# Weight rows of the channel mixers read by TensorE as several regions in turn

## The chip, the cores and the metric

The kernel runs on one core of a Trainium2 chip. The metric is the device time of one execution in microseconds (us). Before the change the median of three runs is 2255.92 us (2255.71 to 2256.01).

## The reference

A decoder trunk of two layers over 256 tokens of 2048 features, in float32. Layer 0 mixes tokens by gated linear attention, layer 1 by forgetting attention; each also attends to 256 memory tokens, and each ends in a channel mixer, the part that this change is about:

```python
def conv_ffn(h, w_up, conv_w, conv_b, w_down):
    u = causal_dwconv(h @ w_up, conv_w, conv_b)
    a, val = split_cols(u, [FFN_HIDDEN, FFN_HIDDEN])
    return (jax.nn.silu(a) * val) @ w_down

def reference(...):
    ...
        h = rmsnorm(x, norm_ffn[i])
        x = x + conv_ffn(h, ffn_w_up[i], ffn_conv_w[i], ffn_conv_b[i], ffn_w_down[i])
```

FFN_HIDDEN is 5632, so h @ w_up is a product of 256 x 2048 by 2048 x 11264, and the second one of 256 x 5632 by 5632 x 2048.

## The kernel before

**A product from three.** TensorE multiplies in the type fp32r. To keep float32's precision, each operand is split into a high part, rounded to fp32r, and a low part, what is left. The activations lie split in SBUF: bufA and bufB, 16 tiles each of 128 features x (high, low) x 256 tokens. A weight tile comes in float32 (raw), ScalarE rounds it (whi, L206), and VectorE takes the difference (wlo, L215). products() (L219 to L231) then adds three matmuls per block of 128 tokens and 128 features into a PSUM bank: high activations by high weights (L227), low activations by high weights (L228), and, behind all of these, high activations by low weights (L231).

**What a matmul reads.** The activations (128 features x 128 tokens) are the stationary operand. The weights are the moving operand: the matmul reads a row of n columns, 512 in the channel mixers, from each of 128 partitions of whi or wlo, from the first column to the last, and writes a row of n columns of PSUM per token.

**Units and panels.** _panels() lists all weights as panels of up to 512 columns, and the host lays them out so that a unit of two blocks of 128 input features by n columns is one DMA of 512 KB (n = 512), 128 partitions x 1024 floats. split_unit() issues load, rounding and difference of a unit; the pools hold four raw tiles, three whi and three wlo. proj_tm() runs one panel through all its units; proj_two() runs two panels side by side. Each unit is used for two blocks of tokens, so a unit is 2 x 2 x 3 = 12 matmuls. The columns of a panel of the form "turned" or "four" are placed by the host in the order SPREAD, so that what comes out of PSUM can be turned on VectorE; that order is the same before and after.

**The channel mixer** (ffn, L864) works in three parts of the hidden features, PARTS = ((0, 16), (16, 32), (32, 44)) in blocks of 128. In each part come the "up" panels (a pair of blocks of both halves each: 8, 8 and 6 panels of 16 blocks of input features), with the convolution and the gate behind them on ScalarE and VectorE, and then four "down" panels (of 16, 16 and 12 blocks), whose results add_out() adds to x on VectorE. Per layer that is 768, 384, 768, 384, 576 and 288 matmuls, in this order. Layer 0's mixer reads bufB for "up" and bufA for "down", layer 1's the other way round. The "down" panels of the last part of layer 1 are the end of the program, before the final norm and the store.

**split()** (L371 to L382) writes a row of 256 tokens as high and low part. With dealt set, it reads its source straight on and writes every other token to the first and to the second half of the row in turn (128 floats apart); without, it writes straight on.

The order of instructions on each engine comes from the program's order and a scheduler with priorities; every weight DMA is on SyncE's queue.

Of the kernel before, what the change touches and what calls it, by code (L numbers as in the profile page):

```python
# [31 lines left out]
PARTS = ((0, 16), (16, 32), (32, 44))  # L32
# [23 lines left out]
def _panels():  # L56

    full = list(range(KC))  # L60
    out = []

    def tm(key, w, c0, n, kcs=full, more=()):
        out.append((key, w, kcs, [(c0, n), *more], 2))

    def turned(key, w, blocks, kcs=full):

        out.append((key, w, kcs, [(blocks, 512)], 2))

    def four(key, w, c0, kcs=full):  # L70
        turned(key, w, [c0 + k * P for k in range(4)], kcs)

    for l in range(2):
        four(("mk", l), ("mem_w_kv", l), 0)
        tm(("mv", l), ("mem_w_kv", l), 512, 512)
    for h in range(GLA_H):
        tm(("gv", h), ("gla_w_in", 0), G_V + h * DV, DV, more=[] if h else [(G_R, RANK)])
        turned(("qk", h), ("gla_w_in", 0), [g + h * DK + k * P for g in (G_Q, G_K) for k in range(2)])
    for j in range(3):
        four(("og", j), ("gla_w_in", 0), G_OG + j * 512)  # L80
    four(("mq", 0), ("gla_w_in", 0), G_MQ)
    late = list(range(12, 16)) + list(range(12))

    def ffn(l):
        for p, (lo, hi) in enumerate(PARTS):
            for j in range(lo, hi, 2):
                turned(("up", l, j), ("ffn_w_up", l), [c + k * P for c in (0, HID) for k in (j, j + 1)])
            for f in range(4):
                four(("down", l, p, f), ("ffn_w_down", l), f * 512, list(range(lo, hi)))

    for f in range(4):
        four(("wo", 0, f), ("gla_w_out", 0), f * 512)
    ffn(0)
    for j in range(3):
        four(("fk", j), ("fox_w_kv", None), F_K + j * 512)
    for j, (lo, hi) in enumerate(FV_PARTS):
        more = [] if j else [(F_L, FOX_H)]
        tm(("fv", j), ("fox_w_kv", None), F_V + lo, hi - lo, more=more)
    four(("mq", 1), ("fox_w_in", 0), FOX_H * HD)
    for j in range(3):  # L100
        four(("fq", j), ("fox_w_in", 0), j * 512)
    for f in range(4):
        four(("wo", 1, f), ("fox_w_out", 0), f * 512, late)
    ffn(1)
    return out


def _layout():

    where, off = {}, 0  # L110
    for key, _, kcs, cols, per in _panels():
        n = sum(c[1] for c in cols)
        units = []
        for u in range(0, len(kcs), per):
            units.append((off, kcs[u : u + per], n))
            off += P * per * n
        where[key] = units
    return where, off
# [17 lines left out]
def _trunk(ctx: ExitStack, tc: tile.TileContext, xt, xtok, memt, wp, wgu, gns, gfin, cnv, par, msk, out):  # L136
    nc = tc.nc
    where, _ = _layout()
    V, S, TE = nc.vector, nc.scalar, nc.tensor
# [69 lines left out]
    def split_unit(unit, pieces=1, before=None, pool=wpool):  # L209
        with tc.high_priority(offset=AHEAD):  # L210
            raw, hi, w = load_unit(unit, pieces, before, pool)
            lo = pool.tile([P, NUNIT], F32R, name="wlo", tag="wlo", bufs=3)
            for i in range(pieces):
                s = slice(i * w // pieces, (i + 1) * w // pieces)
                V.tensor_tensor(lo[:, s], raw[:, s], hi[:, s].bitcast(F32), ALU.subtract)  # L215
        passed()
        return hi, lo

    def products(accs, src, base, unit, hi, lo, first, last):  # L219

        kcs, n = unit[1], unit[2]
        low = []
        for b, acc in accs:
            for j, kc in enumerate(kcs):
                s = slice(j * n, (j + 1) * n)
                xh, xl = (src[kc - base][:, i, b * P : (b + 1) * P] for i in range(2))
                TE.matmul(acc[:, :n], xh, hi[:, s], start=first and j == 0, stop=False)  # L227
                TE.matmul(acc[:, :n], xl, hi[:, s], start=False, stop=False)  # L228
                low.append((acc[:, :n], xh, lo[:, s], last and j == len(kcs) - 1))
        for a, xh, ls, stop in low:  # L230
            TE.matmul(a, xh, ls, start=False, stop=stop)  # L231

    def proj_tm(key, src, evac, spare=None, before=None):

        units = where[key]
        n = units[0][2]
        base = min(min(u[1]) for u in units)
        acc = [pacc.tile([P, 512], F32, name="acc", tag="acc") for _ in range(2)]
        ahead = 0 if spare is None else 4
        ready = {}  # L240
        for i in range(len(units) + ahead):
            if i < len(units):
                pool = wpool if spare is None or i < 3 else spare
                ready[i] = split_unit(units[i], pool=pool) if before is None else before(i, units[i])
            for bs, u in [((0, 1), i)] if not ahead else [((0,), i), ((1,), i - ahead)]:
                if 0 <= u < len(units):
                    products([(b, acc[b]) for b in bs], src, base, units[u], *ready[u], u == 0, u == len(units) - 1)
                    if u == len(units) - 1:
                        for b in bs:
                            evac(b, acc[b][:, :n])  # L250

    def proj_two(keys, src, evacs, late):

        units = [where[k] for k in keys]
        base = min(min(u[1]) for u in units[0])
        acc = [[pacc.tile([P, 512], F32, name="acc", tag="acc") for _ in range(2)] for _ in keys]
        count = len(units[0])
        for part in (range(count - late), range(count - late, count)):
            for i in range(2):
                for u in part:  # L260
                    unit = units[i][u]
                    hi, lo = split_unit(unit)
                    products(list(enumerate(acc[i])), src, base, unit, hi, lo, u == 0, u == count - 1)
                if part[-1] == count - 1:
                    for b in range(2):
                        evacs[i](b, acc[i][b][:, : units[i][0][2]])
# [240 lines left out]
    with tc.tile_pool(name="load", bufs=1) as lp:  # L507
# [31 lines left out]
        def mv_out(l):  # L539
            return to_values(nrm, 512, lambda c: mv[l][:, c, :])  # L540

        proj_tm(("mk", 0), bufA, keys(0), before=first)
        nc.sync.dma_start(mask[:, :M_SCAN], msk[:, :M_SCAN])
        sq, acc = [x[f].rearrange("p b (c t) -> p (b c) t", t=T) for f in range(2)]
# [9 lines left out]
        with tc.issue_after(loads[-1].ins):  # L554
            for i in range(KC):
                nc.sync.dma_start(xf[i], xt[i])
            nc.sync.dma_start(part, par)
            nc.sync.dma_start(mask[:, M_SCAN:], msk[:, M_SCAN:M_FOX])
        proj_tm(("mv", 0), bufA, mv_out(0))
        for i in range(KC):  # L560
            split(bufB, i, xf[i], gain("mix0", i), False)
        proj_tm(("mk", 1), bufA, keys(1))
        with tc.issue_after(loads[-1].ins):
            for f in range(4):
# [186 lines left out]
    def fox(nx, kept, then):  # L751
        hk, hq, mix = bufB, bufA, bufB
        with tc.tile_pool(name="fox", bufs=1) as fp:
# [6 lines left out]
            def keys(j):  # L760
                return to_features([(0, 4, nx.col)], lambda: lambda k: kt[:, 4 * j + k, :])

            proj_two([("fk", j) for j in range(2)], hk, [keys(j) for j in range(2)], 2)

            def queries(f):
# [85 lines left out]
    def add_out(key, src, then=None, spare=None, late=1):  # L851
        def evac(f):
            def out(b, a):
                V.tensor_tensor(x[f][:, b, :], x[f][:, b, :], a, ALU.add)  # L854
                if then is not None:
                    then(f, b)

            return out

        proj_two([(*key, f) for f in range(2)], src, [evac(f) for f in range(2)], late)  # L860
        for f in range(2, 4):
            proj_tm((*key, f), src, evac(f), spare if f == 3 else None)
# [54 lines left out]
    def preparing(name, dst):  # L917
        n = StreamNorm()
        turns = {}

        def then(f, b):
            n.add(f, b)
            if not b:
                turns[f] = Turn("xturned", 4)
            turns[f].put(b, x[f][:, b, :])
            if not b:
                return

            def halves(c):
                def step(t):  # L930
                    for k in (c, c + 1):
                        split(dst, 4 * f + k, t[:, k, :], gain(name, 4 * f + k))

                return step

            transfers(turns[f], back, (9, halves(0)), (10, halves(2)))

        return n, then, turns

    n, then, _ = preparing("ffn0", bufB)  # L940
# [3 lines left out]
    n, then, _ = preparing("ffn1", bufA)  # L944
# [121 lines left out]
```

## Time and profile before

| | |
|---|---|
| runs: median (lowest to highest) | 2255.92 us (2255.71 to 2256.01) |
| the profiled execution's own time | 2254.47 us |
| its span, first to last instruction | 2252.7 us |
| TensorE busy | 2239.9 us, 99% |
| VectorE busy | 1525.7 us, 68% |
| ScalarE busy | 1276.5 us, 57% |
| DMA | 516.96 MB, mean 229 GB/s |
| mean granted TensorE clock | 0.999 |

The tables of the profile name an engine (PE is TensorE's matmuls, PEld its weight loads, DVE VectorE, ACT ScalarE, POOL GpSimd, SP SyncE), a line of the kernel, and out<-in with the program's names and shapes. "x768" is a count; "174.10 (x769)" is busy us and instructions; in a row of a group, the numbers behind the bar are busy us and mean ns of one, then the idle time before it and who ended it. Matmuls overlap in TensorE, so the mean ns of one is longer than the time from one start to the next. Times in stretches are us from the span's start. A row that is timed "A:B" is such a stretch.

### The profile page before, as it was taken

To read this page: it belongs to the slowest core of one execution; us is meant where nothing else is said; L and a number is where in the kernel's file an instruction comes from. 1 tells how busy PE (TensorE), PEld (TensorE's weight loads), DVE (VectorE), ACT (ScalarE), POOL (GpSimd) and SP (SyncE) were. 2 spreads that over 40 slices of the span, in tenths; PEclk is the share of its full clock that TensorE was granted. 3 is DMA by queue.
4 is the path that set the end of the run, shared out by engine and by line. 5 is a ranking of instruction groups with operands and counts; after the bars stand their busy time and mean duration, and the time that the engine had idled before them with its cause. 6 is when DMAs were issued, how large, how long until landed. Compare 5 with 4: busy or idle time off the path is not lost.

```text
span 2252.7 us, 29275 instructions
## 1 busy us (share of the span) xinstructions
PE 2239.9 (99%) x10336; PEld 1874.8 (83%) x10336; DVE 1525.7 (68%) x2317; ACT 1276.5 (57%) x1850; POOL 2.9 (0%) x15
## 2 busy tenths in 40 slices
PE   9999999999999999999999999999999999999998
PEld 7888888888888888888888998888888888888886
DVE  7568988667675576646776556766776467664766
ACT  7555666556553565535665655555655456544654
POOL 0000000000000000000000000000000000000000
PEclk9999999999999999999999999999999999999999
DMA  9875666677775777657777876677776677766774
GB/s 318 279 233 188 207 204 220 205 233 246 250 234 195 227 237 246 209 195 247 234 250 255 257 266 202 181 251 238 244 251 216 196 240 240 242 203 210 239 242 150
DMA packets 303771, 516.96 MB, mean 229 GB/s; under 512 B 178556, under 2 KB 187272, under 8 KB 303496
## 3 DMA queue, kind: packets, MB, share of 16 engines
q1 hardware_dynamic: 124296, 427.24, 57.1%
q10 hardware_dynamic: 179328, 87.85, 13.9%
q8 instruction: 81, 1.33, 0.2%
q14 instruction: 66, 0.54, 0.1%
HBM read 470.44 MB, written 44.58 MB: 229 GB/s over the span
## 4 chain that ended last, share of the span: by engine, by line
PE 98%; DMA 1%; DVE 1%; issue 0%; ACT 0%; SPq 0%; DVEq 0%; ACTq 0%
PE acc L227 32%; PE acc L228 32%; PE acc L231 31%; DMA raw<-wp 0%; PE ps_s L683 0%; PE ps_s L485 0%; PE ps_t L478 0%; PE ps_o L496 0%; DMA xf<-xt 0%; DVE wlo L215 0%; DMA back<-turned 0%; PE ps_s L825 0%; PE ps_o L841 0%; PE ps_o L703 0%; PE ps_s L603 0%
## 5 line engine op out<-in xcount | busy, mean ns | idle before, releaser
L215 DVE TENSOR_TENSOR wlo<-raw,whi 128x1024 fp32r<-128x1024 f32 (+4 forms) x809 | 969.7, 1201 | 636.6 <-ACT whi L206 615.4
L206 ACT ACTIVATE whi<-raw 128x1024 fp32r<-128x1024 f32 (+4 forms) x809 | 842.3, 1043 | 860.0 <-PE acc L228 703.3
L227 PE MATMUL acc<-whi,B 128*128 128x512 f32 (+3 forms) x1792 | 685.7, 384 | 0.0
L228 PE MATMUL acc<-whi,B 128*128 128x512 f32 (+3 forms) x1792 | 684.5, 383 | 0.0
L227 PE MATMUL acc<-whi,A 128*128 128x512 f32 x1440 | 562.3, 392 | 1.4 <-ACT A L378 1.0
L228 PE MATMUL acc<-whi,A 128*128 128x512 f32 x1440 | 559.8, 390 | 0.0
L231 PE MATMUL acc<-wlo,B 128*128 128x512 f32 (+3 forms) x1792 | 469.3, 382 | 0.0
L231 PE MATMUL acc<-wlo,A 128*128 128x512 f32 x1440 | 387.2, 390 | 0.3 <-DVE wlo L215 0.3
L227 PEld LDWEIGHTS acc<-whi,B 128*128 128x128 f32 x1792 | 336.3, 188 | 60.5
L228 PEld LDWEIGHTS acc<-whi,B 128*128 128x128 f32 x1792 | 336.0, 188 | 59.5
L231 PEld LDWEIGHTS acc<-wlo,B 128*128 128x128 f32 x1792 | 333.7, 188 | 59.7
L227 PEld LDWEIGHTS acc<-whi,A 128*128 128x128 f32 x1440 | 270.6, 188 | 60.0 <-ACT whi L206 1.8
L228 PEld LDWEIGHTS acc<-whi,A 128*128 128x128 f32 x1440 | 270.7, 188 | 55.9 <-DVE A L382 0.2
L231 PEld LDWEIGHTS acc<-wlo,A 128*128 128x128 f32 x1440 | 270.0, 188 | 56.6 <-DVE wlo L215 0.7
L881 ACT ACTIVATE cv<-u,cw 128x256 f32<-128x256 f32 x176 | 96.9, 589 | 22.9 <-DMA u<-turned 22.9
L882 DVE SCALAR_TENSOR_TENSOR cv<-u,cw,cv 128x256 f32<-128x256 f32 x176 | 78.2, 479 | 14.9 <-ACT cv L881 14.9
L298 DVE STREAM_TRANSPOSE square<-scaled 128x512 f32<-128x512 f32 x122 | 80.0, 691 | 0.0
L883 DVE SCALAR_TENSOR_TENSOR cv<-u,cw,cv 128x256 f32<-128x256 f32 x176 | 77.1, 479 | 0.0
L854 DVE TENSOR_TENSOR x<-x,acc 128x512 f32<-128x512 f32 x64 | 41.2, 681 | 22.7 <-PE acc L231 22.7
L896 ACT ACTIVATE scaled<-acc,ny 128x512 f32<-128x512 f32 x88 | 54.8, 674 | 0.0
L462 ACT ACTIVATE sq<-x 128x256 f32<-128x256 f32 x80 | 32.5, 408 | 15.4 <-DVE x L854 14.0
L886 DVE TENSOR_TENSOR cv<-cv,cv 128x256 f32<-128x256 f32 x88 | 37.3, 424 | 1.4 <-ACT cv L885 1.4
(179 smaller groups left out, 846.3 us busy)
## 6 DMA issues: line engine op xcount, KB each, us to landing
raw<-wp SPq DMA_DIRECT2D x743, 512.0 KB, 4.2
turned<-square ACTq DMA_DIRECT2D x61, 512.0 KB, 4.5
u<-turned ACTq DMA_DIRECT2D x176, 128.0 KB, 5.2
raw<-wp SPq DMA_DIRECT2D x32, 384.0 KB, 3.1
raw<-wp SPq DMA_DIRECT2D x24, 388.0 KB, 4.5
back<-xturned ACTq DMA_DIRECT2D x64, 128.0 KB, 5.1
xturned<-square ACTq DMA_DIRECT2D x12, 512.0 KB, 4.4
back<-turned ACTq DMA_DIRECT2D x32, 128.0 KB, 4.2
```

The source lines that it names most:

```text
L206: casts.append(S.activation(hi[:, s], raw[:, s], AF.Copy))
L215: V.tensor_tensor(lo[:, s], raw[:, s], hi[:, s].bitcast(F32), ALU.subtract)
L227: TE.matmul(acc[:, :n], xh, hi[:, s], start=first and j == 0, stop=False)
L228: TE.matmul(acc[:, :n], xl, hi[:, s], start=False, stop=False)
L231: TE.matmul(a, xh, ls, start=False, stop=stop)
L298: V.transpose(self.square[:, :, :, b], src.rearrange("p (c t) -> p c t", t=32))
L854: V.tensor_tensor(x[f][:, b, :], x[f][:, b, :], a, ALU.add)
L881: S.activation(r, v[:, 2:], AF.Identity, bias=w[3], scale=w[2])
L882: V.scalar_tensor_tensor(r, v[:, 1 : T + 1], w[1], r, ALU.mult, ALU.add)
L883: V.scalar_tensor_tensor(r, v[:, :T], w[0], r, ALU.mult, ALU.add)
L886: V.tensor_tensor(cv[1], cv[0], cv[1], ALU.mult)
L896: S.activation(e, a, AF.Copy, scale=nx.col()[:, b : b + 1])
```

## The change

A table gives a form (s, t) for each part of each layer's "up" and "down" panels. The row of 512 floats is taken as s regions of 512 / s floats. A matmul reads t floats from the first region, t from the second, and so on through all s, then the next t of the first. The host places the columns so that what is read in this order is what was read straight on before; so PSUM gets the same columns in the same order, and the results are as before. All three matmuls read so. ScalarE and VectorE still write whi and wlo straight on, the DMAs are the same in number, size and order, and on every engine the same instructions stand in the same order with the same waits. The other panels (attention, memory, their output projections) have no form and are read straight on.

| part | up, layer 0 | down, layer 0 | up, layer 1 | down, layer 1 |
|---|---|---|---|---|
| 0 | 2 regions, runs of 16 | 4, 16 | 2, 32 | 8, 4 |
| 1 | 2, 4 | 2, 8 | 2, 128 | 8, 16 |
| 2 | 2, 64 | 4, 4 | 4, 32 | 2, 2 |

```diff
+RUNS = {
+    ("up", 0, 0): (2, 16), ("up", 0, 1): (2, 4), ("up", 0, 2): (2, 64),
+    ("down", 0, 0): (4, 16), ("down", 0, 1): (2, 8), ("down", 0, 2): (4, 4),
+    ("up", 1, 0): (2, 32), ("up", 1, 1): (2, 128), ("up", 1, 2): (4, 32),
+    ("down", 1, 0): (8, 4), ("down", 1, 1): (8, 16), ("down", 1, 2): (2, 2),
+}
+
+
+def _runs(key):
+    if key[0] == "up":
+        key = (*key[:2], next(p for p, (lo, hi) in enumerate(PARTS) if lo <= key[2] < hi))
+    return RUNS.get(key[:3])
...
-    def products(accs, src, base, unit, hi, lo, first, last):
+    def products(accs, src, base, unit, hi, lo, first, last, runs=None):
 
         kcs, n = unit[1], unit[2]
+
+        def moving(t):
+            return t if runs is None else t.rearrange("p (s g t) -> p g s t", s=runs[0], t=runs[1])
+
         low = []
         for b, acc in accs:
             for j, kc in enumerate(kcs):
                 s = slice(j * n, (j + 1) * n)
                 xh, xl = (src[kc - base][:, i, b * P : (b + 1) * P] for i in range(2))
-                TE.matmul(acc[:, :n], xh, hi[:, s], start=first and j == 0, stop=False)
-                TE.matmul(acc[:, :n], xl, hi[:, s], start=False, stop=False)
-                low.append((acc[:, :n], xh, lo[:, s], last and j == len(kcs) - 1))
+                TE.matmul(acc[:, :n], xh, moving(hi[:, s]), start=first and j == 0, stop=False)
+                TE.matmul(acc[:, :n], xl, moving(hi[:, s]), start=False, stop=False)
+                low.append((acc[:, :n], xh, moving(lo[:, s]), last and j == len(kcs) - 1))
...
             at = np.empty(512, np.int64)
             at[SPREAD] = np.concatenate([np.arange(c, c + P) for c in cols[0][0]])
+            if _runs(key) is not None:
+                s, r = _runs(key)
+                at = at.reshape(-1, s, r).transpose(1, 0, 2).reshape(-1)
             blk = w3[kcs][:, :, at]
```

proj_tm() and proj_two() pass the form of their panel to products().

More of the change, by code (lines that the diff above doesn't have):

```diff
@@ L246, in proj_tm @@
                 if 0 <= u < len(units):
-                    products([(b, acc[b]) for b in bs], src, base, units[u], *ready[u], u == 0, u == len(units) - 1)
+                    products([(b, acc[b]) for b in bs], src, base, units[u], *ready[u], u == 0, u == len(units) - 1, _runs(key))
                     if u == len(units) - 1:
@@ L262, in proj_two @@
                     hi, lo = split_unit(unit)
-                    products(list(enumerate(acc[i])), src, base, unit, hi, lo, u == 0, u == count - 1)
+                    products(list(enumerate(acc[i])), src, base, unit, hi, lo, u == 0, u == count - 1, _runs(keys[i]))
                 if part[-1] == count - 1:
```

## The prediction

> **What bounds the kernel now.** First the page of the profile: the busy time of each engine, and the chain that ended last.
>
> ```profile
> PE 2239.9 (99%) x10336; PEld 1874.8 (83%) x10336; DVE 1525.7 (68%) x2317; ACT 1276.5 (57%) x1850; POOL 2.9 (0%) x15
> ...
> PE 98%; DMA 1%; DVE 1%; issue 0%; ACT 0%; SPq 0%; DVEq 0%; ACTq 0%
> PE acc L227 32%; PE acc L228 32%; PE acc L231 31%; DMA raw<-wp 0%; PE ps_s L683 0%; PE ps_s L485 0%; PE ps_t L478 0%; PE ps_o L496 0%; DMA xf<-xt 0%; DVE wlo L215 0%; DMA back<-turned 0%; PE ps_s L825 0%; PE ps_o L841 0%; PE ps_o L703 0%; PE ps_s L603 0%
> ```
>
> The chain is TensorE's own queue: 98% of it, and 95% are the three matmuls of products(), the lines that the diff edits. A busy TensorE says little by itself, so the next view is the table of stretches of time, cut where the timeline shows products() change from one buffer of activations to the other: the twelve parts of the channel mixers in their order (layer 0 up, down, up, down, up, down, then layer 1). Columns: stretch, its length, busy time and instructions of TensorE, of its weight load, of VectorE and of ScalarE, GpSimd, granted clock, DMA share, GB/s.
>
> ```profile
> 469.80:643.90 174.10, 174.10 (x769) 144.14 (x768) 124.61 (x186) 105.13 (x147) 0.00 (x0) 1.00 0.75 242
> 643.90:730.94 87.04, 87.04 (x385) 72.10 (x384) 49.34 (x55) 39.30 (x44) 0.00 (x0) 1.00 0.62 206
> 730.94:905.02 174.08, 174.08 (x769) 144.19 (x768) 118.90 (x163) 100.50 (x134) 0.00 (x0) 1.00 0.73 235
> ...
> 992.06:1122.62 130.56, 130.56 (x577) 108.14 (x576) 87.75 (x119) 74.12 (x98) 0.00 (x0) 1.00 0.73 233
> 1122.62:1187.90 65.28, 65.28 (x289) 54.07 (x288) 46.94 (x62) 39.57 (x68) 0.31 (x1) 1.00 0.80 255
> ...
> 1698.88:1785.92 87.04, 87.04 (x385) 72.10 (x384) 49.36 (x55) 39.29 (x44) 0.00 (x0) 1.00 0.64 206
> ...
> 2177.60:2243.10 65.50, 65.50 (x289) 53.90 (x287) 43.59 (x62) 35.80 (x65) 0.00 (x0) 1.00 0.52 169
> ```
>
> Busy time equals length in every row: TensorE has no hole, at a granted clock of 1.00. The pace is the same everywhere: 174.08 / 768 = 87.04 / 384 = 65.28 / 288 = 0.2267 us from one matmul's start to the next. So no weight tile is late, VectorE and ScalarE are done early (124.6 and 105.1 of 174.1 us at most), and any nanosecond that a matmul gains or loses here reaches the end in full. The view of waits agrees; TensorE's two largest in the whole span are
>
> ```profile
> PE ps_o L172 <- DVE B L169: 1.4, 1, 1.4
> PE acc L227 <- ACT A L378: 1.0, 2, 0.7
> ```
>
> of which the first is before any product. A stretch of the forgetting layer with 384 columns per matmul splits the pace into its parts (16.67 us for 96 matmuls):
>
> ```profile
> 1304.60:1321.27 16.67, 16.67 (x98) 16.67 (x97) 9.40 (x10) 8.51 (x11) 0.00 (x0) 1.00 0.90 303
> ```
>
> 16.67 / 96 = 173.6 ns for 384 columns against 226.7 for 512: (226.7 - 173.6) / 128 = 0.415 ns per column, and 226.7 - 512 x 0.415 = 14 ns that do not depend on the width. TensorE takes a float from each row of the weight tile every 0.415 ns.
>
> **The change part by part.** Every instruction stays in its place on its engine, with its waits; the weight DMAs (512 KB each), the split on ScalarE and VectorE and the writes to PSUM keep their shapes. Only the order in which a matmul reads its 512 weights differs: by the table of stretches, 768 + 384 + 768 + 384 + 576 + 288 = 3168 matmuls per layer, 6336 in all, 1436 us of the 2252.7. All else I cost at nothing: the host's new column order is no device time, and the loads and splits that hide behind TensorE now would hide better behind a slower one. If TensorE became faster, VectorE's 124.6 of 174.1 us leaves room for 28%.
>
> The price of a jump between regions is not in the trace for these matmuls. The one TensorE operation that reads two runs (L636, runs of 64 columns) stands beside one of the same width in one run:
>
> ```profile
> L824 PE MATMUL ps_s<-fkt,back 128*128 128x128 f32 x24 | 4.6, 273 | 0.0
> L636 PE MATMUL ps_s<-gq,gk 128*128 128x128 f32 x16 | 2.4, 274 | 0.0
> ```
>
> 274 against 273 ns: one jump costs 1 ns at most, and long runs look free. For short runs the nearest rows are those of split(), where ScalarE and VectorE write the halves of a token row in turn, one float to each of two regions 128 floats apart (L381 and L382 from back), or straight on (the same lines from xf):
>
> ```profile
> L381 ACT ACTIVATE B<-back,gains 128x256 fp32r<-128x256 f32 x32 | 20.2, 746 | 0.5 <-DMA back<-xturned 0.5
> L381 ACT ACTIVATE B<-xf,gains 128x256 fp32r<-128x256 f32 x16 | 6.8, 498 | 0.0
> L382 DVE SCALAR_TENSOR_TENSOR B<-back,gains,B 128x256 fp32r<-128x256 f32 x32 | 19.3, 681 | 0.0
> L382 DVE SCALAR_TENSOR_TENSOR B<-xf,gains,B 128x256 fp32r<-128x256 f32 x16 | 6.6, 479 | 0.0
> ...
> L206 ACT ACTIVATE whi<-raw 128x1024 fp32r<-128x1024 f32 x743 | 786.7, 1060 | 794.8 <-PE acc L228 655.2 <-ACT cv L885 40.6 <-PE acc L231 28.5
> L206 ACT ACTIVATE whi<-raw 128x768 fp32r<-128x768 f32 x32 | 26.9, 846 | 31.3 <-PE acc L228 22.7 <-issue 2.8 <-DMA raw<-wp 2.1
> ```
>
> ScalarE: (746 - 498) / 256 = 0.97 ns more per float, on a pace of (1060 - 846) / 256 = 0.84, so a visit to a region lasts about 1.8 ns. VectorE: (681 - 479) / 256 = 0.79 more. Two engines of different pace both need some 1.7 to 1.8 ns per visit, which looks like a time of the memory and not of the engine. TensorE's straight read sets a bound of its own: four adjacent floats in 4 x 0.415 = 1.66 ns. I take 1.66 ns as the least time of a visit for TensorE too. Then, per form:
>
> - Runs of 8 to 128 last 3.3 ns and more: the jump hides. Eight of the twelve forms, 4608 matmuls, nothing.
> - Runs of 4 last 1.66 ns, just the visit. Layer 0 up part 1 (768 matmuls), layer 0 down part 2 (288), layer 1 down part 0 (384): 1440 matmuls, taken at nothing. With ScalarE's 1.8 ns a visit would be 0.14 too long: 0.14 x 128 jumps x 1440 = 26 us, the upper end of this term.
> - Runs of 2 last 0.83 ns, half a visit. Layer 1 down part 2, 288 matmuls of 256 visits: (1.66 - 0.83) x 256 = 212 ns more per matmul, 227 to 439 ns, and 212 x 288 = 61.2 us. With 1.8 ns: 0.97 x 256 x 288 = 71.5 us. The lower end is nothing (below).
>
> That last part is the end of the program. Its stretch grows from 65.5 to 127 us, with the tail of 9.6 us behind it as it is; the weights come sooner relative to use, so nothing new is late. **The sum:** the profiled execution took 2254.47 us (span 2252.7); 2254.5 + 61.2 = 2315.7. The timed runs lie at 2255.71 to 2256.01, 1.5 us above it, less than the sum is worth: **2316**, which is +2.7%. The forecast's own range is 2312 to 2355 (71.5 + 26 on top at most).
>
> [...]
>
> **The rivals.** *No form costs anything.* VectorE's rows speak for it: the transposes of L298 write every second float of a row, L854 all of them, 512 each:
>
> ```profile
> L298 DVE STREAM_TRANSPOSE square<-scaled 128x512 f32<-128x512 f32 x122 | 80.0, 691 | 0.0
> L854 DVE TENSOR_TENSOR x<-x,acc 128x512 f32<-128x512 f32 x64 | 41.2, 681 | 22.7 <-PE acc L231 22.7
> ```
>
> [...] Against it: VectorE moves a float in about 1.04 ns (the 1223 and 956 ns of its two widths of L215, 267 / 256), TensorE in 0.415, so what is hidden there need not be hidden here. Time: 2254.5 to 2256. [...]
>
> ```profile
> L215 DVE TENSOR_TENSOR wlo<-raw,whi 128x1024 fp32r<-128x1024 f32 x743 | 907.2, 1223 | 587.4 <-ACT whi L206 575.9 <-DMA raw<-wp 3.2 <-PE ps_s L603 2.9
> L215 DVE TENSOR_TENSOR wlo<-raw,whi 128x768 fp32r<-128x768 f32 x32 | 30.2, 956 | 16.5 <-ACT whi L206 11.5 <-PE acc L231 4.9
> ```
>
> *Short jumps cost whether or not the run is long enough.* If neighbouring floats are fetched ahead and a jump breaks that, a run of 4 pays too: at 0.79 to 0.97 ns per jump 128 x 1440 jumps are 146 to 179 us, with the pairs' 58 to 72 on top 2458 to 2505; half hidden, 2356 to 2380. If every jump of all forms pays (361,000 of them: 512 / run x matmuls, summed over the twelve) it is 285 to 350 us, 2540 to 2605. L636 speaks against the last, though at half the pace.
>
> *A fixed cost per matmul* for the longer pattern, taken as ScalarE's step of 0.84 ns: 6336 x 0.84 = 5 us, 2260. L636's 1 ns allows it, no more.
>
> *Faster.* 14 ns of each 226.7 do not come from the columns. If they are the wait for the first floats of the next row, which a straight read finds in the same place as the last ones of the row before, then regions in turn would spread them, and the stages of 2, 4 or 8 regions would run below 226.7 ns: all of it in every stage would be 14 x 6336 = 89 us, 2166; in the 768 matmuls of 8 regions alone 11 us, 2244. It decides from 0.7 ns per matmul on (0.2% of 2254 / 6336). Against it: the 14 ns are the same to 0.1% in every stage before, whatever tile is read, which does not look like a collision of addresses.
>
> **How the numbers follow.** Forecast (pairs halved, quads up to a little) 0.42; no cost 0.31; jumps cost at quads too, or everywhere 0.16; fixed cost 0.07; faster 0.04. Together the forecast, no cost and the fixed cost hold 0.80, from 2250 (no cost, with some room for the timing) to 2355; the half-hidden case of quads reaches 2380, and since the price of a quad is the least known number I take 2390 as upper end. A measurement of this kernel tells about 0.2% (4.5 us) from no change: faster 0.04; same 0.33 (no cost, and a little of the fixed cost); slower 0.63.
>
> **What would show it.** In the profile after, the last part of layer 1 (down, 288 matmuls) should take about 127 us instead of 65.5 and start where it did, at 2177.6; every other part should keep its 0.2267 us per matmul. If that part too keeps it, pairs are free and the visit's time isn't the memory's. [...] A part below its length of before would be the faster rival. The forecast is wrong from the start if ScalarE's and VectorE's doubled time per float is a matter of writing, since TensorE only reads here.

## The result, and the profile after

The changed kernel takes 2370.18 us (median; 2369.74 to 2370.91) against 2255.82 us before (2254.86 to 2256.01): a ratio of 1.0508, 95% interval 1.049 to 1.0526, 114 us more. The profiled execution has a span of 2368.7 us.

The page of the profile after: busy time of each engine, and the chain that ended last by engine.

```profile
PE 2354.9 (99%) x10336; PEld 1885.8 (80%) x10336; DVE 1531.9 (65%) x2317; ACT 1283.7 (54%) x1850; POOL 2.9 (0%) x15
...
PE 97%; DMA 1%; DVE 1%; issue 0%; ACT 0%; SPq 0%; ACTq 0%; DVEq 0%
```

TensorE is still the whole chain. Its busy time grew by 115.0 us; VectorE's and ScalarE's by 6 and 7 us, behind a TensorE that stays busy for 99% of the span. So the matmuls are slower, not later. The same table of stretches as before, cut where the parts begin now (layer 0 up, down, up, down, up, down, then layer 1):

```profile
469.89:654.21 184.32, 184.32 (x770) 145.92 (x769) 125.60 (x186) 105.88 (x147) 0.00 (x0) 1.00 0.72 228
654.21:742.97 88.76, 88.76 (x385) 72.19 (x384) 49.38 (x54) 39.28 (x44) 0.00 (x0) 1.00 0.62 202
742.97:934.97 192.00, 192.00 (x770) 145.15 (x768) 121.03 (x163) 103.17 (x134) 0.00 (x0) 1.00 0.65 214
934.97:1028.41 93.44, 93.44 (x385) 72.77 (x384) 49.49 (x54) 39.25 (x44) 0.00 (x0) 1.00 0.56 191
1028.41:1159.01 130.60, 130.60 (x577) 108.14 (x576) 87.62 (x119) 74.01 (x98) 0.00 (x0) 1.00 0.73 233
1159.01:1236.20 77.19, 77.19 (x290) 56.19 (x288) 47.63 (x62) 40.70 (x68) 0.32 (x1) 1.00 0.69 222
1574.28:1756.05 181.77, 181.77 (x770) 145.23 (x769) 125.51 (x186) 106.01 (x147) 0.00 (x0) 1.00 0.73 232
1756.05:1862.81 106.76, 106.76 (x385) 73.93 (x384) 49.80 (x54) 40.87 (x44) 0.00 (x0) 1.00 0.52 169
1862.81:2036.92 174.11, 174.11 (x769) 144.15 (x768) 118.79 (x163) 100.32 (x134) 0.00 (x0) 1.00 0.74 235
2036.92:2128.88 91.96, 91.96 (x385) 72.83 (x384) 49.43 (x55) 39.32 (x44) 0.00 (x0) 1.00 0.60 195
2128.88:2263.29 134.41, 134.41 (x578) 108.13 (x576) 88.25 (x119) 74.07 (x98) 0.00 (x0) 1.00 0.72 227
2263.29:2359.08 95.79, 95.79 (x289) 55.97 (x287) 44.42 (x61) 36.29 (x65) 0.00 (x0) 1.00 0.37 122
```

Every part is still without a hole (busy equals length, clock 1.00), so length / matmuls is the pace of each form. Divided by 768, 384, 768, 384, 576 and 288 and set against 226.7 ns; the last column is the part's length less its length before:

| form (regions, run) | ns per matmul | extra ns | part's extra us |
|---|---|---|---|
| 2, 2 | 332.6 | 106 | 30.3 |
| 8, 4 | 278.0 | 51.4 | 19.7 |
| 4, 4 | 268.0 | 41.4 | 11.9 |
| 2, 4 | 250.0 | 23.3 | 17.9 |
| 2, 8 | 243.3 | 16.7 | 6.4 |
| 2, 16 | 240.0 | 13.3 | 10.2 |
| 8, 16 | 239.5 | 12.8 | 4.9 |
| 2, 32 | 236.7 | 10.0 | 7.7 |
| 4, 32 | 233.4 | 6.7 | 3.9 |
| 4, 16 | 231.1 | 4.5 | 1.7 |
| 2, 64 and 2, 128 | 226.7 | 0.1 | 0.1 |

The twelve add up to 114.7 us of the 116.0 us between the two profiled spans (2368.7 and 2252.7): the change lies in the pace of its matmuls.

### The profile page after: what moved, and what is told of

It reads as the page before. It is cut to its first block, busy times and chain, and to the rows that moved or that the text cites. A ratio compares the mean times of both kernels' runs of the same rounds, so it can differ in the third digit from the quotient of the medians.

```text
span 2368.7 us, 29275 instructions
## 1 busy us (share of the span) xinstructions
PE 2354.9 (99%) x10336; PEld 1885.8 (80%) x10336; DVE 1531.9 (65%) x2317; ACT 1283.7 (54%) x1850; POOL 2.9 (0%) x15
## 4 chain that ended last, share of the span: by engine, by line
PE 97%; DMA 1%; DVE 1%; issue 0%; ACT 0%; SPq 0%; ACTq 0%; DVEq 0%
PE acc L246 31%; PE acc L245 31%; PE acc L249 31%; DMA xturned<-square 1%; DMA raw<-wp 0%; PE ps_s L701 0%; PE ps_s L503 0%; PE ps_t L496 0%; PE ps_o L514 0%; DVE wlo L229 0%; DMA back<-turned 0%; PE ps_s L843 0%; PE ps_o L859 0%; PE ps_o L721 0%; DVE B L400 0%
## 5 line engine op out<-in xcount | busy, mean ns | idle before, releaser
L245 PE MATMUL acc<-whi,B 128*128 128x512 f32 (+3 forms) x1792 | 714.9, 400 | 0.9 <-ACT whi L220 0.9
L246 PE MATMUL acc<-whi,B 128*128 128x512 f32 (+3 forms) x1792 | 715.3, 400 | 0.0
L245 PE MATMUL acc<-whi,A 128*128 128x512 f32 x1440 | 572.7, 399 | 1.5 <-ACT A L396 1.0
L246 PE MATMUL acc<-whi,A 128*128 128x512 f32 x1440 | 571.3, 398 | 0.0
L249 PE MATMUL acc<-wlo,B 128*128 128x512 f32 (+3 forms) x1792 | 497.6, 399 | 0.0
L245 PEld LDWEIGHTS acc<-whi,B 128*128 128x128 f32 x1792 | 338.5, 189 | 85.7 <-ACT whi L220 1.3
L249 PE MATMUL acc<-wlo,A 128*128 128x512 f32 x1440 | 397.9, 398 | 0.3 <-DVE wlo L229 0.3
L245 PEld LDWEIGHTS acc<-whi,A 128*128 128x128 f32 x1440 | 272.4, 189 | 69.6 <-ACT whi L220 1.9
```

What stands on the lines that cost most here:

```text
L245: TE.matmul(acc[:, :n], xh, moving(hi[:, s]), start=first and j == 0, stop=False)
L246: TE.matmul(acc[:, :n], xl, moving(hi[:, s]), start=False, stop=False)
```

## The experiments

Four theories stood against each other. **A**, the prediction's: a visit to a region has a least time. **B**: each jump costs a tick, by which is meant the time of one column: in the stretch of 384 columns of before, 90 starts of matmuls in a row take 15.60 us (1304.80 to 1320.40), 173.3 ns each, and (226.7 - 173.3) / 128 = 0.417 ns. **C**: the distance in memory decides. **L**, formed after the first batch: the floats at even and at odd places of a row go through two readers, and each wants several floats in a row from the same 16 bytes. The readers are a picture of the author's; a trace shows only what an order of reading takes.

### Other forms

```diff
-    ("up", 0, 0): (2, 16), ("up", 0, 1): (2, 4), ("up", 0, 2): (2, 64),
-    ("down", 0, 0): (4, 16), ("down", 0, 1): (2, 8), ("down", 0, 2): (4, 4),
+    ("up", 0, 0): (2, 1), ("up", 0, 1): (8, 1), ("up", 0, 2): (4, 2),
+    ("down", 0, 0): (8, 2), ("down", 0, 1): (128, 2), ("down", 0, 2): (16, 4),
...
+    ("up", 1, 0): (64, 4), ("up", 1, 1): (4, 8), ("up", 1, 2): (8, 8),
+    ("down", 1, 0): (8, 32), ("down", 1, 1): (4, 64), ("down", 1, 2): (8, 64),
```

> Other forms in the twelve parts: runs of 1 in 2 and 8 regions, runs of 2 in 4, 8 and 128, of 4 in 16 and 64, of 8 in 4 and 8, of 32 in 8, of 64 in 4 and 8. Times are from one matmul's start to the next (226.7 ns straight on). Theory A, the one of the prediction, corrected to the pairs' measured 1.25 ns: a visit to a region has a least time, and a longer run hides it. Then runs of 1 take 512 x 1.25 + 13 = 653 ns, runs of 2 take 333 ns with any number of regions, all others 226.7. Theory B: each jump costs one tick of TensorE, 0.417 ns, whatever the run. Then runs of 1 take 440 ns, of 2 333, of 4 280, of 8 253, of 32 233, of 64 230. Theory C: the cost hangs on the places in memory that a jump joins. Then runs of one length differ with the number of regions: those with short steps forward (2 in 128 regions steps 4 floats, 4 in 64 regions steps 8 floats) are cheaper than 333 and 280, and 8 regions of runs of 8 dearer than 2 regions were (243).

The table of stretches of this kernel, layer 0 up part 0 (2, 1), down part 0 (8, 2), up part 1 (8, 1), down part 1 (128, 2), up part 2 (4, 2), and layer 1 up part 0 (64, 4) and up part 1 (4, 8):

```profile
470.15:635.91 165.76, 165.76 (x769) 145.15 (x768) 121.21 (x178) 100.85 (x142) 0.00 (x0) 1.00 0.81 250
635.91:822.88 186.97, 186.97 (x386) 79.86 (x384) 54.84 (x63) 42.80 (x49) 0.00 (x0) 1.00 0.32 101
822.88:1196.64 373.76, 373.76 (x770) 159.74 (x768) 121.12 (x162) 103.17 (x134) 0.00 (x0) 1.00 0.34 110
1196.64:1369.87 173.23, 173.23 (x386) 79.49 (x385) 50.33 (x54) 38.69 (x42) 0.00 (x0) 1.00 0.32 103
1369.87:1625.23 255.36, 255.36 (x578) 118.66 (x576) 88.91 (x118) 75.05 (x98) 0.00 (x0) 1.00 0.38 119
...
2034.55:2212.05 177.50, 177.50 (x770) 144.26 (x769) 125.08 (x186) 105.92 (x147) 0.00 (x0) 1.00 0.76 237
...
2302.92:2480.43 177.51, 177.51 (x769) 144.19 (x768) 119.15 (x163) 100.76 (x134) 0.00 (x0) 1.00 0.75 231
```

Singles in two regions take 165.76 / 768 = **215.8 ns, 10.8 less than a straight read**. No theory had that. Singles in 8 regions take 486.7, pairs in 4 and 8 regions 443.3 and 486.9, runs of 4 in 64 regions 231.1, of 8 in 4 regions 231.1. A falls (the shortest visits of all are the fastest), B falls with it, and the number of regions matters, as C says. But C's order does not hold either: pairs with short steps forward (128 regions) should be under 333 and take 451.1, runs of 8 in 8 regions should be above 243 and take 233.8. The other forms: runs of 4 in 16 regions 246.7, runs of 32 in 8 regions 236.6, runs of 64 in 4 regions 226.8, as straight on.

### The same forms in other parts

```diff
-    ("up", 0, 0): (2, 16), ("up", 0, 1): (2, 4), ("up", 0, 2): (2, 64),
+    ("up", 0, 0): (2, 2), ("up", 0, 1): (8, 4), ("up", 0, 2): (8, 16),
...
-    ("down", 1, 0): (8, 4), ("down", 1, 1): (8, 16), ("down", 1, 2): (2, 2),
+    ("down", 1, 0): (2, 64), ("down", 1, 1): (2, 16), ("down", 1, 2): (2, 4),
```

> The same twelve forms, each moved to the other layer, from up to down or back, and to another part. If the form makes the cost (A, B and C all say so), each form keeps its ns per matmul to 1 ns: 333 for pairs, 278 for runs of 4 in 8 regions, 268 in 4, 250 in 2, and 226.7 for runs of 64 and 128. Since up parts have twice the matmuls of down parts, the total follows from the counts: sum of matmuls times the extra ns, +186 us, so a span near 2439 us. If the place in the program makes it (other tiles of activations, other neighbours on ScalarE and VectorE), the costs stay with the parts and the span stays near 2369.

The stretches of layer 0's first up part, now (2, 2), and of layer 1's, now (4, 4):

```profile
469.63:730.74 261.11, 261.11 (x770) 151.88 (x769) 126.77 (x186) 107.04 (x148) 0.00 (x0) 1.00 0.51 163
...
1664.96:1870.78 205.82, 205.82 (x769) 150.15 (x768) 126.71 (x186) 107.70 (x147) 0.00 (x0) 1.00 0.65 205
```

340.0 and 268.0 ns: eleven forms keep their price to 0.2 ns, pairs cost 340 here and 333 there. The form makes the cost, with 2% of place in the pairs. The span is 2449.2 us; the 10 us above the expected come about half from that, and half from the expected sum, which was added up wrongly (the table's extras times the new counts give 191.3, not 186). Why pairs differ by place stays open.

### Regions moved apart

```diff
-            casts.append(S.activation(hi[:, s], raw[:, s], AF.Copy))
+            if runs is None or runs[2] == 0:
+                casts.append(S.activation(hi[:, s], raw[:, s], AF.Copy))
+            else:
+                casts.append(S.activation(regions(hi, w, runs), raw[:, :w].rearrange("p (m n) -> p m n", n=512 // runs[0]), AF.Copy))
```

and the same for wlo and for what the matmul reads; regions() takes the first 512 / s floats of each stretch that is longer by the gap.

> Two regions throughout, but the second is moved away from the first by 4 to 48 floats more (runs of 4: 4, 8, 16, 32, 48; runs of 16: 8, 16, 32; runs of 32: 16, 32; runs of 2: 4, and 1, where its pairs start on an odd float). ScalarE and VectorE write with the gap; three raw tiles in place of four make room, so a few late tiles may show, but not in the median of the matmuls. Theories A and B know no addresses: runs of 4 stay at 250 ns, of 16 at 240, of 32 at 236.7, of 2 at 333. Theory C: the costs change with the distance, since all distances of the forms so far are powers of two; for some distance runs of 4 and 16 fall to 226.7.

The first row is runs of 4 moved by 4 floats, the second by 32, the third runs of 32 moved by 32:

```profile
474.13:664.43 190.30, 190.30 (x769) 145.22 (x768) 131.38 (x190) 110.70 (x150) 0.00 (x0) 1.00 0.72 224
664.43:756.61 92.18, 92.18 (x386) 72.71 (x385) 49.48 (x54) 39.27 (x44) 0.00 (x0) 1.00 0.60 194
...
2173.11:2307.52 134.41, 134.41 (x577) 108.17 (x576) 88.17 (x119) 73.97 (x97) 0.00 (x0) 1.00 0.72 224
```

Runs of 4 take 247.8, 242.2, 241.7, 240.0 and 243.3 ns with gaps of 4, 8, 16, 32 and 48 (250.0 without), runs of 16 take 243.9, 241.1 and 240.0 (240.0), runs of 32 take 241.1 and 233.4 (236.7), pairs 328.0 and, with the second region starting on an odd float, 331.3 (332.6). The distance shifts a price by up to 10 ns, but no distance tried takes it away: neither "no addresses" nor C's strong form holds.

### Fewer columns

```diff
-                TE.matmul(acc[:, :n], xl, moving(hi[:, s]), start=False, stop=False)
-                low.append((acc[:, :n], xh, moving(lo[:, s]), last and j == len(kcs) - 1))
+                TE.matmul(acc[:, :w], xl, part(hi[:, s]), start=False, stop=False)
+                low.append((acc[:, :w], xh, part(lo[:, s]), last and j == len(kcs) - 1))
```

with w = 384, and the L245 matmul likewise except for the first of a sum.

> The forms as changed, but all matmuls of the channel mixers except the first of each sum read only 384 of the 512 columns, so a quarter of the products is left out; layer 1 up part 1 reads straight on as the measure (173.3 ns). It tells whether the 13.3 ns between two matmuls hide a part of the cost. If they don't, the extra is in proportion to the columns, 3/4 of what it was at 512: runs of 2 +80 ns, 4 in 8 regions +38, 4 in 4 regions +31, 4 in 2 regions +17.5, 8 in 2 +12.5, 16 in 2 +10, 16 in 8 +9.6, 32 in 2 +7.5, 32 in 4 +5, 16 in 4 +3.4. If they hide 13.3 ns of it per matmul, the extra is 3/4 of (extra + 13.3) less 13.3: +76.5, +35, +28, +14, +9, +6.7, +6.3, +4.2, +1.7, 0.

The stretches of layer 0 up part 0 (2, 16), down part 1 (2, 8) and of layer 1 down part 0 (8, 4) and part 2 (2, 2):

```profile
469.79:620.32 150.53, 143.23 (x770) 137.21 (x768) 120.10 (x179) 100.45 (x142) 0.00 (x0) 1.00 0.85 274
...
838.85:909.73 70.88, 70.88 (x385) 70.45 (x385) 52.58 (x63) 41.06 (x48) 0.00 (x0) 1.00 0.80 259
...
1570.04:1652.04 82.00, 82.00 (x385) 75.31 (x385) 54.12 (x63) 44.16 (x49) 0.00 (x0) 0.98 0.71 226
...
1981.59:2055.22 73.63, 73.63 (x289) 56.10 (x288) 46.53 (x62) 37.79 (x66) 0.00 (x0) 1.00 0.51 164
```

Inconclusive for most: the shorter matmuls leave holes (143.23 us busy of 150.53, at a DMA share of 0.85), which blur the pace; that late weights make them is the author's reading, and no view names the waits. The part read straight on has holes too, so the 173.6 ns of the stretch of 384 columns before serve as the measure. Three parts are without a hole. Pairs take 255.7 ns, 82 more, of which some 2 are the first matmuls of the sums (8 of 288, still 512 wide): in proportion (80), nothing hidden. Runs of 4 in 8 regions take 213.5, 40 more, some 1 of it from the first matmuls: near the 38 in proportion, though at a granted clock of 0.98. Runs of 8 take 184.6, 11 more, between the 12.5 and the 9 expected.

### Singles in all twelve parts, and in every product

```diff
-RUNS = {
-    ("up", 0, 0): (2, 16), ("up", 0, 1): (2, 4), ("up", 0, 2): (2, 64),
...
+    return 2, 1
...
+        s, r = _runs(key)
+        blk = blk[:, :, np.arange(blk.shape[2]).reshape(-1, s, r).transpose(1, 0, 2).reshape(-1)]
```

This is the second kernel, where all panels have the form (2, 1); the first has (2, 1) in the twelve entries of RUNS and nothing else changed.

> All twelve parts read two regions one float at a time, the form that took 215.8 ns per matmul in the grid. If that form is faster than a straight read by itself (theory L: TensorE reads the odd and the even floats of a row through two readers, each of which keeps its own place in memory; two regions in runs of one give each reader a straight row of its own), all twelve parts come down by 10.8 ns: 6336 x 10.83 = 68.6 us, 2187 us, ratio 0.970. If it was that part of the program only (layer 0 up part 0), the gain is at most that part's 8.3 us, 2248 us. If the faster matmuls run into late tiles (VectorE was busy for 125 of 174 us there), stalls take back a part, and show as matmuls far above the others.

> Every product reads so, the attention's and the memory's too, with the host's order to match. If theory L holds and nothing else is late: 9696 matmuls x 10.8 ns = 105 us, 2151 us, ratio 0.953; somewhat less where TensorE waits for its weight loads (the panels of 384 columns had their weight loads busy all the time, 173.6 ns per matmul; if these bind, 480 matmuls or so keep their time and it is 2156). If the gap is a share of the columns and not fixed, the 384-column matmuls gain 8.1 ns in place of 10.8.

The first took 2187.15 us against 2254.73 of before on the same chip: ratio **0.9701** (0.9686 to 0.9715), 67.6 us less, as expected. The second took 2155.5 us: **0.9563** (0.9547 to 0.9579), 99 us less than before, 4.5 us short of the 2151 expected, and the fastest version. Its first up and down parts of layer 0, and its stretch of 384 columns:

```profile
448.97:616.91 167.94, 167.17 (x770) 144.48 (x768) 121.44 (x178) 100.33 (x141) 0.00 (x0) 1.00 0.79 250
616.91:700.66 83.75, 83.71 (x385) 72.36 (x385) 54.36 (x64) 42.15 (x50) 0.00 (x0) 1.00 0.69 223
```

```profile
1248.30:1263.90 15.60, 15.60 (x98) 15.60 (x97) 9.74 (x11) 8.70 (x12) 0.00 (x0) 1.00 0.92 316
```

The table of TensorE's waits names what has grown (0.2 us for whi and 0.3 for wlo before):

```profile
PE acc L235 <- ACT whi L210: 2.5, 6, 0.6
...
PE acc L239 <- DVE wlo L219: 0.7, 2, 0.6
```

At 215.8 ns the first part would be 165.76 us. It is 2.2 us longer, of which 0.77 are holes (167.17 busy of 167.94). The view, of the whole span, does not say which waits lie in it, and the rest is not explained. 15.60 us for 96 matmuls of 384 columns are 162.5 ns, 11 less than before, about as much less as at 512: the gain is fixed per matmul, and the weight loads, busy all the time (16.67 of 16.67 us before, 15.60 of 15.60 now), did not set the 173.6 ns. From the two widths, (215.83 - 162.5) / 128 = 0.4167 ns per column, which leaves 2.5 ns per matmul for singles; at the same pace per column the straight read's 226.7 leave 13.3.

### Singles from nearer places

```diff
-            return t if runs is None else t.rearrange("p (s g t) -> p g s t", s=runs[0], t=runs[1])
+            return t if runs is None else t.rearrange("p (b s g) -> p b g s", s=runs[1], b=512 // runs[0])
```

> One float at a time, from other places: two halves of a block of 4, 8, 16, 32, 64, 128 and 256 floats, block after block; then 4, 16, 128 and 256 regions over the whole row; and two regions again in another part of the program (layer 1 down part 2). Theory L: each reader needs some floats of the same 16 bytes in a row. Blocks of 8 and more give each reader four in a row, so 215.8 ns from 8 on; blocks of 4 put both readers on the same 16 bytes with two floats each, as straight on, 226.7; 4 and 16 regions make each reader jump at every float, 333 ns or more; 256 regions (every second float, then the others) give each reader one float per 16 bytes, 333 or more; 128 likewise. Theory D (distance: the two floats must lie far apart): 226.7 or more for small blocks, and a step down to 215.8 at some size. Control: the last part 215.8 in either.

Stretches of blocks of 4, of blocks of 8, of 128 regions, and of 4 regions:

```profile
469.44:643.52 174.08, 174.08 (x769) 144.19 (x768) 124.81 (x186) 105.74 (x147) 0.00 (x0) 1.00 0.76 242
...
726.40:892.16 165.76, 165.76 (x769) 145.15 (x768) 116.36 (x160) 97.98 (x132) 0.00 (x0) 1.00 0.78 245
...
1666.81:1843.94 177.13, 177.13 (x385) 80.00 (x384) 53.45 (x61) 41.06 (x47) 0.00 (x0) 1.00 0.33 107
1843.94:2053.88 209.94, 209.94 (x769) 145.56 (x768) 120.56 (x162) 100.40 (x133) 0.00 (x0) 1.00 0.61 194
```

Blocks of 4 take 226.7 ns, blocks of 8 and of every size above 215.8 (the part with blocks of 128 takes 223.9, with 63.00 us busy of 64.48; no view names what it waited for). That is L to the block: in a block of 8, read 0 4 1 5 2 6 3 7, the even places come from floats 0 to 3 and the odd ones from 4 to 7; in a block of 4 both come from the same four. Distance (D) is out. So is a reader that merely keeps a few places at hand: pairs and singles in two regions take the same eight floats from the same two places of 16 bytes within eight reads, in another order, and cost 332.6 and 215.8 ns. Singles in 16, 128 and 256 regions take 435, 461 and 451. L does not say how dear a form is: singles in 4 regions take 273, under the 333 expected, and under the 278 of runs of 4 in 8 regions, which L ranks as the better form.

### Runs that start between multiples of 16 bytes

```diff
+    def regions(t, runs):
+        s, _, pad, off = runs
+        t = t[:, off : off + 1152].rearrange("p (j q) -> p j q", q=576)[:, :, : 512 + s * pad]
+        return t.rearrange("p j (s q) -> p j s q", s=s)[:, :, :, : 512 // s]
```

> Where runs start within 16 bytes. Rows read straight on from 1, 2 and 3 floats past a multiple of 16; runs of 4 in 2 and 8 regions and of 16 in 2, all from 2 floats past; and two regions in singles with the second moved by 1, 2, 4, 16 and 32 floats, or both by 1. ScalarE and VectorE write at the same offset; three raw tiles, so late tiles may show above the median. Theory L with 16 bytes as the place that a reader keeps: a run of 4 from 2 floats past gives each reader one float of one place and one of the next, so it costs as pairs do, 333 ns in 2 regions and more in 8 (against 250 and 278 on 16 bytes); singles give each reader a straight row wherever it starts, 215.8 in all six; straight rows 226.7 or a tick more. If the place is 8 bytes, or a jump is what costs, the runs of 4 keep 250 and 278.

The stretches of straight rows from 1 float past, of runs of 4 in 8, of 16 in 2 and of 4 in 2 regions, all from 2 floats past, and of singles with the second region moved by 1:

```profile
474.30:656.06 181.76, 181.76 (x770) 144.09 (x769) 127.57 (x189) 107.60 (x149) 0.00 (x0) 1.00 0.75 235
656.06:845.47 189.41, 189.41 (x386) 80.61 (x384) 50.43 (x54) 39.72 (x44) 0.00 (x0) 1.00 0.31 97
...
1024.69:1139.88 115.19, 115.19 (x385) 75.55 (x384) 49.77 (x54) 39.68 (x44) 0.00 (x0) 1.00 0.49 158
1139.88:1330.63 190.75, 190.75 (x578) 113.80 (x576) 89.20 (x119) 74.07 (x99) 0.00 (x0) 1.00 0.50 161
...
1733.86:1899.62 165.76, 165.76 (x769) 145.15 (x768) 122.27 (x180) 102.52 (x144) 0.00 (x0) 1.00 0.81 253
```

Runs of 4 in 2 regions go from 250 to 331 ns, the price of pairs, and in 8 regions from 278 to 493. The jumps are the same in number and distance; only where they fall within 16 bytes has changed. Singles stay at 215.8 to 216.7 wherever they start. That settles the 16 bytes against 8, and against the jump as such. Straight rows pay a little for a start off 16 bytes: 236.7, 233.4 and 228.9 ns from 1, 2 and 3 floats past. Runs of 16 go from 240 to 300 ns. L has them dearer, but not by this much: 73 / 32 = 2.3 ns per jump, against 104 / 128 = 0.8 for runs of 4 from the same start.

### Only forward

```diff
+            if runs is not None and runs[0] == 0:
+                return t.rearrange("p (g j t) -> p j g t", j=2, t=runs[1])[:, j]
```

> Layer 0: the two blocks of a unit lie in turn in runs of t floats, and a matmul reads t, skips t and so on, always forward, t from 2 to 64; layer 1 has the changed kernel's forms. If the jump itself costs (theory B), the same number of jumps costs as in 2 regions: 250 ns for runs of 4, 243 of 8, 240 of 16, 236.7 of 32, 333 of 2. If the way back and forth between far places costs (theory C), skipping forward costs less: 226.7 to 231 from runs of 4 on, as 64 regions did (231). Runs of 2 stay dear in either, 333 or more: each reader gets one float per 16 bytes. Layer 1 as changed.

Layer 0's runs of 4, 32, 2 and 16, skipping forward:

```profile
469.41:648.60 179.19, 179.19 (x769) 144.15 (x768) 125.17 (x186) 106.07 (x147) 0.00 (x0) 1.00 0.75 235
648.60:739.89 91.29, 91.29 (x385) 72.27 (x384) 49.43 (x54) 39.32 (x44) 0.00 (x0) 1.00 0.62 197
...
918.25:1092.31 174.06, 174.06 (x385) 79.61 (x384) 50.33 (x54) 39.61 (x44) 0.00 (x0) 1.00 0.33 106
1092.31:1230.89 138.58, 138.58 (x578) 108.49 (x576) 88.27 (x119) 73.84 (x97) 0.00 (x0) 1.00 0.69 216
```

Neither theory takes all. Runs of 4 and 8 are cheaper forward (233.3 and 232.2 for 250.0 and 243.3), so there the way back and forth is most of the price: 16.7 of 23.3 ns, and 11.1 of 16.6. Runs of 16 and 32 cost what they did (240.6 and 237.7), so there the price goes with the jump. Runs of 64 are free (226.7). Pairs are dearer forward, 453 for 333: forward, a matmul reads one half of each 16 bytes; back and forth, it reads the second half two floats after the first. Whether that makes the difference was not shown.

## Why the prediction was right in its range and wrong in its sum

The time lies in the range (2250 to 2390) and the direction was forecast, but 2370 is not the 2316 of the likeliest case, nor within that case's own range to 2355. It lies in the stated range because that was stretched for a rival, half-hidden jumps, and because two errors partly offset each other: 31 us too much for the pairs, 84 us too little for the rest. That part is luck.

- *What bounds it.* Right: no hole in any part, and the extra of the matmuls, 114.7 us in the profile, is the 114.4 us between the medians. All that was costed at nothing on the other engines cost nothing.
- *"I take 1.66 ns as the least time of a visit for TensorE too."* This is the step that failed. Singles in two regions visit one every 0.42 ns (215.8 / 512) and are the fastest form. That a visit takes as long as four floats was the author's estimate; no run shows it. The rows it was taken from, ScalarE and VectorE writing one float to each of two regions, say nothing of TensorE's reading; the prediction named that doubt last and priced it nowhere.
- *Runs of 2, +61.2 us.* Measured 30.3: a pair costs 106 / 256 = 0.41 ns, half of the 0.83. Dear, as forecast, though not for the reason given; by L, each reader gets one float per 16 bytes and visit.
- *Runs of 4, nothing, 26 us at most.* Measured 17.9 + 11.9 + 19.7 = 49.5 us, and more with more regions (23, 41, 51 ns with 2, 4 and 8), which a least time per visit can't give. The factor between runs of 4 and of 16 comes out as 1.8, 9 and 4 for 2, 4 and 8 regions, where a price per jump alone would make it 4 in all.
- *Runs of 8 to 128, nothing.* Right for 64 and 128 (226.7 ns). The six forms of 8 to 32 cost 34.8 us. L636, two runs of 64 (274 against 273 ns), was a true witness for runs of 64, and for no shorter one.
- *No form costs anything.* Pairs cost 106 ns a matmul. The rows that spoke for it, L298 and L854 (691 and 681 ns), are VectorE's, and do not say what TensorE pays. What fits these runs better is several floats from the same 16 bytes for each of the even and the odd places, and that is not enough either: runs of 4 on 16 bytes have them, and pay 23 to 51 ns, against 104 and 267 from two floats past.
- *The rivals.* Nearest in time came "short jumps cost whether or not the run is long enough, half hidden" (2356 to 2380, in a case given 0.16), in part by chance: it has 73 to 90 us for runs of 4, which cost 49.5, and nothing for runs of 8 to 32, which cost 34.8; its 29 to 36 us for the pairs fit. "Faster" was right about where a gain could be and wrong about the forms: 10.8 of the 14 ns that the prediction found besides the columns go away, but with singles, which the change doesn't have. Its counter-argument, that 14 ns everywhere alike do not look like a matter of addresses, was weak: a cost that is the same everywhere may be the same because the pattern is.

**Shown**: the cost belongs to the form (moved; the pairs to 2%), it turns in the main on whether the floats at even and at odd places come several at a time from the same 16 bytes (blocks of 4 and 8, 226.7 and 215.8 ns; runs of 4 from two floats past, 331 for 250), and singles in two regions by themselves yield a gain (67.6 us in the twelve parts). That there are two readers is the simplest picture that the author found to fit; no run shows them. **Open**: what sets the size of a price (singles in 4 regions, runs of 16 from two floats past); why jumps at runs of 16 and 32 cost some 0.4 to 0.7 ns each at most distances (13.3 / 32, 10.0 / 16, skipping forward 13.9 / 32 and 11.0 / 16) and at runs of 64 nothing; what makes the price of a distance; and why a straight read has 13.3 ns besides its columns and singles 2.5.

## What to carry to other kernels

Where TensorE reads fp32r rows without a hole, as here, the order in which a row lies in SBUF had a price: keep runs of 64 floats and more (226.7 ns, as straight on), start rows on 16 bytes (straight rows that start off them take 228.9 to 236.7, runs of 4 in 2 regions 331 for 250), and avoid pairs (328 to 487). Where the host lays the weights anyway, deal neighbours of a row to two places at least four floats apart (215.8 ns in blocks of 8, 226.7 in blocks of 4), so that even and odd places read straight rows of their own; here singles in two regions gave 4.4% in all products. An unexplained fixed remainder in the pace of the bounding instruction deserves one cheap survey of many forms in one run before it is called fixed.

## What was not expected of the hardware

A straight read of 512 fp32r columns is not TensorE's fastest: 226.7 ns against 215.8 for two interleaved halves, 173.6 against 162.5 at 384 columns, at the same granted clock of 1.00. The interleaving may be as local as 8 floats (215.8). And a price can jump by 81 ns per matmul (250 to 331) when the same pattern starts 8 bytes later.
